# A PEER feed-forward kernel on one Trainium2 core: the gates of the last two token blocks are handed to the first expert tiles on chip, gate flushes run on across token tiles, and 40 activation tiles are spilled in place of 42

## The chip, the core and the metric

The kernel runs on one core of one Trainium2 chip. The metric is the device time of one execution in microseconds (us). The kernel before takes 3240.67 us, the median of 3 runs (3237.8 to 3242.23).

## What is computed

A trunk of two residual layers on 512 tokens of width 1024. Each layer has a token mixer (attention with pooling, then attention with a recurrence) and a PEER feed-forward: 8 heads choose 16 of 16,384 single-neuron experts for each token. Only this last part is touched:

```python
q  = (xt @ w_query).reshape(n_tok, 8, 2, 128)
s1 = einsum('thd,nd->thn', q[:, :, 0], sub_k1); s2 = einsum('thd,nd->thn', q[:, :, 1], sub_k2)
v1, i1 = top_k(s1, 16); v2, i2 = top_k(s2, 16)          # first-level choice
cand = v1[..., :, None] + v2[..., None, :]
top_s, pos = top_k(cand.reshape(n_tok, 8, 256), 16)     # second-level choice
idx  = take_along_axis(i1 * 128 + i2, pos); gate = softmax(top_s)
act  = gelu(einsum('thkd,td->thk', expert_u[idx], x))
out  = einsum('thk,thkd->td', gate * act, expert_v[idx])
```

## The kernel before

The function `peer` does this part in each layer. For 384 of the 512 tokens (three token tiles of 128) it computes all 16,384 experts densely, as 128 expert tiles of 128 experts; the last 128 tokens gather the rows of their chosen experts one by one (`g_fetch`, `g_work`, lines 1721 to 1747).

**u side.** `u_step(j)` makes the activations of expert tile j: it fetches the weights of tile j+5 (`ur`, SP's queue, line 1359), rounds those of tile j+3 (`uh`, ACT), makes the remainder of tile j+2 (`ul`, DVE, line 1374), runs 24 matmuls of 384 columns on PE (lines 182 to 184) and takes the gelu on ACT. The first 12 tiles stay on chip; the next `NB_SPILL` are written to memory (`ad`, line 1385) and read back on the v side; the rest are made there.

**Second-level choice and gates.** `level2(t)` (lines 1500 to 1567) makes the chosen pairs and gates of token tile t on DVE. It ends with three PE transposes into `pkT`, which ACT copies to `pT`. `gates(t)` (lines 1569 to 1611) spreads them over all experts in 8 blocks of 16 tokens. For each block DVE builds four one-hot tensors (`ohC`, `ohA`, `ohB` twice, line 1604); a `flush` is 8 small matmuls on PE into `gps` (line 1587) and one copy by ACT into `gs` (line 1589); four flushes fill a block, which ACT's queue then writes to memory (`gd`, line 1591). Flushes trail by up to four, and each `gates(t)` empties its list before it returns (lines 1608 and 1609).

**The order around it.** `background()` is a hand-written interleaving. Every piece of `level2` and `gates` yields a cost; after each 4.2 of cost (`G_STEP`) one `u_step` is put in, up to `NB_ACT + NB_SPILL - NB_LAST` = 49. Pieces of `level2(t+1)` are mixed into `gates(t)` (line 1619). Steps 49 to 51 follow, then the pools of this stage are closed (line 1640) and the v side takes their memory.

**v side.** `V(j)`, as the text calls `v_mm(j)`, is 18 matmuls of 512 columns on PE into six accumulators (line 1704). It needs `vh` and `vl` (`v_load`: fetched `vr`, rounded on ACT, remainder on DVE) and `Hh` and `Hl` (`h_make`: activation times gate, `Hf`, on DVE line 1685, then split). The gates come back from memory as `gt`, for 8 expert tiles at a time (`g_load`, line 1656). Ahead of the loop stand `g_load(0)` with all 24 blocks, three `vr` fetches, `v_load(0)`, step 52, `h_make(0)` and step 53. In round j below 42 of the loop only V(j) runs on PE; after that each round has a u step and a V. `units` spreads the gathered rows of the last tokens over the rounds.

Every transfer of the SP and ACT queues takes the next of eight completion counters in turn, and its issue waits until the transfer eight places before it has landed.

Of the kernel before, what the change touches and what calls it, by code (L numbers as in the profile page):

```python
# [1316 lines left out]
GJ = 8  # L1317
G_STEP = 4.2
NB_ACT = 12
NB_SPILL = 42  # L1320
ROWS = 5
ADA_M = 12
TAIL = NE - 2
NB_LAST = 5


def peer(k, layer):
    nc, tc = k.nc, k.tc
    I = k.I
    with ExitStack() as st:  # L1330
# [20 lines left out]

        up = st.enter_context(tc.tile_pool(name="pu", bufs=2, reuse_waits="tile"))
        ap = st.enter_context(tc.tile_pool(name="pact", bufs=NB_ACT, reuse_waits="tile"))
        U, ACTS = {}, {}

        def u_fetch(j):
# [128 lines left out]
        nc.vector.tensor_copy(IF, IX)  # L1485
        wk = tk.enter_context(tc.tile_pool(name="pwk", bufs=1, reuse_waits="tile"))
        psG = tk.enter_context(tc.tile_pool(name="psG", bufs=6, space=PSUM, reuse_waits="tile"))
        PK = {}

        def tree(m, out):  # L1490

# [8 lines left out]
        def level2(t):  # L1500
            v1, v2 = V[:, t, 0], V[:, t, 1]
            x1, x2 = IF[:, t, 0], IF[:, t, 1]
            cand = wk.tile([P, 8, NCAND], F32, name="cand")
            d1 = wk.tile([P, 8, 16], F16, name="d1")
            nc.vector.tensor_tensor(d1[:, :, 1:16], x1[:, :, 1:16], x1[:, :, 0:15], op=ALU.subtract)
            nc.vector.tensor_copy(d1[:, :, 0:1], x1[:, :, 0:1])
            o = 0
            for a0, na, nb in SEGS:
                dst = cand[:, :, o:o + na * nb].rearrange("p h (a b) -> p h a b", a=na)
                nc.vector.tensor_tensor(dst, bc(v1[:, :, a0:a0 + na, None], [P, 8, na, nb]),  # L1510
                                        bc(v2[:, :, None, 0:nb], [P, 8, na, nb]), op=ALU.add)
                o += na * nb
            yield 2.0
            tv = wk.tile([P, 8, 16], F32, name="tv")
            tp = wk.tile([P, 8, 16], U32, name="tp")
            cr = wk.tile([P, 8, NCAND], F32, name="cr")
            for h in (0, 4):
                top16([(tv[:, i], tp[:, i], cand[:, i, :], cr[:, i, :]) for i in range(h, h + 4)])
                yield 2.4
            d1x = wk.tile([P, 16, 8, 16], F16, name="d1x", tag="dx")  # L1520
            k.act(d1x, bc(d1.rearrange("p h a -> p a h")[:, :, :, None], [P, 16, 8, 16]), AF.Copy)
            pk = wk.tile([P, 3, P], F32, name="pk", bufs=2)
            ge = wk.tile([P, 8, 16], F32, name="ge")
            nc.vector.tensor_tensor(ge, tv, bc(tv[:, :, 0:1], [P, 8, 16]), op=ALU.subtract)
            k.act(ge, ge, AF.Exp)
            pf = wk.tile([P, P], F16, name="pf")
            nc.vector.tensor_copy(pf, tp.rearrange("p h k -> p (h k)"))

            c1 = wk.tile([P, 16, P], F16, name="c1")
            m1 = wk.tile([P, 16, P], F16, name="m1")  # L1530
            nc.vector.tensor_tensor(c1, bc(pf[:, None, :], [P, 16, P]), startx, op=ALU.is_ge)
            yield 1.6
            nc.vector.tensor_tensor(m1, c1, d1x.rearrange("p a h k -> p a (h k)"), op=ALU.mult)
            yield 1.1
            tree(m1, pk[:, 0])
            yield 1.3
            x2x = wk.tile([P, 16, 8, 16], F16, name="x2x", tag="dx")
            k.act(x2x, bc(x2.rearrange("p h a -> p a h")[:, :, :, None], [P, 16, 8, 16]), AF.Copy)
            nc.vector.tensor_tensor(m1, c1, dsx, op=ALU.mult)
            yield 1.1  # L1540
            bb = wk.tile([P, P], F16, name="bb")
            tree(m1, bb)
            nc.vector.tensor_tensor(bb, pf, bb, op=ALU.subtract)
            yield 1.5
            nc.vector.tensor_tensor(c1.rearrange("p a (c t) -> p a c t", t=2),
                                    bc(bb.rearrange("p (c t) -> p c t", t=2)[:, None], [P, 16, 64, 2]),
                                    bc(iotax[:, 0:16, None, :], [P, 16, 64, 2]), op=ALU.is_equal)
            yield 1.1
            nc.vector.tensor_tensor(m1, c1, x2x.rearrange("p a h k -> p a (h k)"), op=ALU.mult)
            yield 1.1  # L1550
            tree(m1, pk[:, 1])
            gs = wk.tile([P, 8], F32, name="gs")
            nc.vector.tensor_reduce(gs, ge, axis=AX.X, op=ALU.add)
            nc.vector.reciprocal(gs, gs)
            nc.vector.tensor_scalar(gs, gs, GSCALE, None, op0=ALU.mult)
            nc.vector.tensor_tensor(pk[:, 2].rearrange("p (h k) -> p h k", h=8), ge, bc(gs[:, :, None], [P, 8, 16]),
                                    op=ALU.mult)
            yield 2.0
            PK[t] = pk
            if t < NTD:  # L1560

                ps = psG.tile([P, 4, P], F32, name="pkT", tag="g")
                for i in range(3):
                    nc.tensor.transpose(ps[:, i, :], pk[:, i], cst(k, "ident"))
                pT = wk.tile([P, 4, P], F16, name="pT", bufs=2)
                k.act(pT[:, 0:3], ps[:, 0:3], AF.Copy)
                PK[t] = (pT, ps)

        def gates(t):
# [7 lines left out]
            pT, ps = pk  # L1577
            nc.vector.tensor_tensor(pT[:, 3], ps[:, 2], pT[:, 2], op=ALU.subtract)
            yield 0.3
            pend = []  # L1580

            def flush():
                A, B, gs, blk, q = pend.pop(0)
                ps = psG.tile([P, 4, P], F32, name="gps", tag="g")
                for i in range(4):
                    for r in range(2):
                        nc.tensor.matmul(ps[:, i, :], A[:, 2 * q + i // 2, :, i % 2], B[r][:, 2 * q + i // 2, :, i % 2],  # L1587
                                         start=r == 0, stop=r == 1, skip_group_check=True)
                k.act(gs[:, :, 4 * q:4 * q + 4].rearrange("p j t -> p t j"), ps, AF.Copy, scale=1.0 / GSCALE)
                if q == GB // 4 - 1:  # L1590
                    nc.scalar.dma_start(gd[blk], gs)


            iota = bc(iotax[:, None], [P, GB // 2, P, 2])
            for b in range(P // GB):
                gs = wk.tile([P, NE, GB], F32, name="gs_", bufs=2)
                C, A = (wk.tile([P, GB // 2, P, 2], F16, name=nm, bufs=n) for nm, n in (("ohC", 1), ("ohA", 3)))
                B = [wk.tile([P, GB // 2, P, 2], F16, name="ohB", bufs=4) for _ in range(2)]

                def pt(i):  # L1600
                    return bc(pT[:, i, b * GB:b * GB + GB].rearrange("p (q t) -> p q t", t=2)[:, :, None, :], [P, GB // 2, P, 2])

                for out, a, i, op in ((C, iota, 1, ALU.is_equal), (A, iota, 0, ALU.is_equal), (B[0], C, 2, ALU.mult), (B[1], C, 3, ALU.mult)):
                    nc.vector.tensor_tensor(out, a, pt(i), op=op)
                    if len(pend) > 3:
                        flush()
                    yield 1.2
                pend += [(A, B, gs, t * (P // GB) + b, q) for q in range(GB // 4)]
            while pend:
                flush()  # L1610
            yield 0.1

        def background():
            yield from level2(0)
            for t in range(3):
                g = level2(t + 1)
                for i, cost in enumerate(gates(t)):
                    yield cost
                    if 12 * (i + 1) // 31 > 12 * i // 31:
                        yield next(g, 0.0)  # L1620
                yield from g
            yield from gates(3)
# [8 lines left out]
        for cost in background():  # L1631
            debt += cost
            if debt >= G_STEP and ju < NB_ACT + NB_SPILL - NB_LAST:
                debt -= G_STEP
                u_step(ju)
                ju += 1
        while ju < NB_ACT + NB_SPILL - 2:
            u_step(ju)
            ju += 1
        tk.close()  # L1640


        with ExitStack() as st2:
            vp = st2.enter_context(tc.tile_pool(name="pv", bufs=2, reuse_waits="tile"))
            psO = st2.enter_context(tc.tile_pool(name="psO", bufs=1, space=PSUM, reuse_waits="tile"))
            O_ = [[psO.tile([P, 512], F32, name=f"o{t}{b}") for b in range(2)] for t in range(NTD)]
            VV, GG, HH = {}, {}, {}

            def g_load(j, parts):

# [31 lines left out]
            def h_make(j):  # L1682
                g = GG[j // GJ]
                hf = vp.tile([P, TD], F32, name="Hf", bufs=1)
                nc.vector.tensor_tensor(hf.rearrange("p (b t) -> p b t", t=GB),
                                        ACTS.pop(j).rearrange("p (b t) -> p b t", t=GB), g[:, :, j % GJ, :], op=ALU.mult)
                if j == NE - 1:

                    h, l = (up.tile([P, TD], F32R, name="acts", bufs=3) for _ in range(2))
# [14 lines left out]
                            mm(O_[t][b], w[:, ts], v[:, 512 * b:512 * b + 512], start=s, stop=e, skip_group_check=True)  # L1704


            acc = vp.tile([P, D], F32, name="gacc", bufs=1)
            nc.vector.memset(acc, 0.0)
            ops = []
            for c in range(P + 20):  # L1710
# [100 lines left out]
                nc.sync.dma_start(k.O["out_0_dram"][t * P:t * P + P, :], o)  # L1811


            g_load(0, range(6))
            for _ in range(3):
                v_fetch()
            v_load(0)
            while ju < NB_ACT + NB_SPILL:
                if ju == NB_ACT + NB_SPILL - 1:
                    h_make(0)  # L1820
                u_step(ju)
                ju += 1
# [230 lines left out]
```

## Time and profile before

| | |
|---|---|
| median of 3 runs | 3240.67 us |
| the profiled execution, its own time | 3234.92 us |
| its span, first to last instruction | 3233.2 us |
| PE busy | 3125.4 us, 97% |
| DVE busy | 2421.7 us, 75% |
| ACT busy | 1410.6 us, 44% |
[...]
| share of PE in the chain that ended last | 84% |

PE is busy almost everywhere, so a change shows where PE waits or runs at a lower clock. The views below are: busy time of each engine in a stretch, waits (who waited for whom), the timeline of one engine, the chain that ended last, and the landing times of transfers. Layer 0's stage of gates ends near 652 us and its v side begins at 686.5 us; in layer 1 the same places are near 2338 and 2373 us.

### The profile page before, as it was taken

Reading aid. Unit: us, or ns where it says so; the run is one execution under the profiler, and the core shown is the slowest. Engines: PE = TensorE matmul, PEld = TensorE weight load, DVE = VectorE, ACT = ScalarE, POOL = GpSimd, SP = SyncE. Lnnn points to the kernel's source line nnn. Section 1 sums busy time; section 2 is a strip of 40 time slices with the busy share of each in tenths; the row PEclk is TensorE's granted clock in tenths of the full one; section 3 lists DMA queues with packets and bytes.
Section 4 is the critical chain, followed back from the end, with each engine's and each line's share of the span. In section 5 each row is a group of like instructions: output and inputs, shape, how many; then the busy total and the mean of one; then the engine's idle time right before and its main releaser. Section 6 shows DMA issues by size and latency. Waiting matters only on the chain.

```text
span 3233.2 us, 55219 instructions
## 1 busy us (share of the span) xinstructions
PE 3125.4 (97%) x21696; PEld 2736.8 (85%) x21696; DVE 2421.7 (75%) x4749; ACT 1410.6 (44%) x1959; POOL 856.8 (27%) x671
## 2 busy tenths in 40 slices
PE   7999999989999999999999899999989999999998
PEld 5777899978899999997677787899978899999997
DVE  5255799957888888887565456899957888888886
ACT  3253367743333333333444533367733333333334
POOL 0002200013444444442020103100013344444442
PEclk8999999999999999999999999999999999999999
DMA  8523246789999999995521014256799999999994
GB/s 313 209 92 139 99 159 248 249 306 349 331 331 343 334 336 331 336 337 178 209 67 53 6 61 163 95 183 231 265 316 342 328 336 338 337 333 333 341 328 146
DMA packets 321830, 794.27 MB, mean 246 GB/s; under 512 B 26400, under 2 KB 162976, under 8 KB 309280
## 3 DMA queue, kind: packets, MB, share of 16 engines
q1 hardware_dynamic: 225968, 439.53, 39.5%
q0 software_dynamic: 75008, 274.78, 24.1%
q10 hardware_dynamic: 20592, 76.43, 6.3%
q8 instruction: 170, 2.79, 0.4%
q14 instruction: 92, 0.75, 0.1%
HBM read 715.36 MB, written 75.24 MB: 245 GB/s over the span
## 4 chain that ended last, share of the span: by engine, by line
PE 84%; DVE 8%; ACT 3%; DMA 3%; issue 2%; ACTq 0%; POOL 0%; DVEq 0%; SPq 0%
PE o L1704 31%; PE ups L182 9%; PE ups L184 9%; PE ups L183 9%; PE bk L182 3%; PE bk L184 3%; PE bk L183 3%; PE bk L745 2%; PE gps L1587 2%; PE qps L182 2%; PE adaps L242 1%; PE qps L183 1%; PE qps L184 1%; PE qps L429 1%; DVE ul L1374 1%
## 5 line engine op out<-in xcount | busy, mean ns | idle before, releaser
L182 PE MATMUL ups<-phh,uh 128*128 128x384 f32 x2048 | 694.6, 339 | 0.0
L184 PE MATMUL ups<-phh,ul 128*128 128x384 f32 x2048 | 689.3, 337 | 0.0
L183 PE MATMUL ups<-phl,uh 128*128 128x384 f32 x2048 | 687.9, 336 | 0.0
L1726 POOL DMA_INDIRECT row<-peer_u,xres x256 | 348.1, 1360 | 1098.1 <-PE gps L1587 552.7
L151 ACT ACTIVATE vh<-vr 128x1024 fp32r<-128x1024 f32 x254 | 269.9, 1063 | 553.7 <-issue 457.0
L1704 PE MATMUL o<-vh,Hh 128*128 128x512 f32 x1524 | 475.1, 393 | 20.7 <-ACT Hh L151 20.6
L1704 PE MATMUL o<-vl,Hh 128*128 128x512 f32 x1524 | 472.7, 391 | 0.0
L1704 PE MATMUL o<-vh,Hl 128*128 128x512 f32 x1524 | 472.4, 391 | 0.0
L1726 POOL DMA_INDIRECT row<-peer_v,xres x256 | 342.9, 1340 | 417.8 <-DVE xres L1742 330.1
L182 PEld LDWEIGHTS ups<-phh,uh 128*128 128x128 f32 x2048 | 386.5, 189 | 5.8
L176 DVE TENSOR_TENSOR vl<-vr,vh 128x1024 fp32r<-128x1024 f32 x254 | 311.1, 1225 | 107.1 <-ACT vh L151 102.6
L183 PEld LDWEIGHTS ups<-phl,uh 128*128 128x128 f32 x2048 | 386.3, 189 | 5.8
L184 PEld LDWEIGHTS ups<-phh,ul 128*128 128x128 f32 x2048 | 385.9, 188 | 0.8 <-DVE ul L1374 0.6
L1704 PEld LDWEIGHTS o<-vh,Hh 128*128 128x128 f32 x1524 | 284.0, 189 | 72.9 <-ACT Hh L151 24.0
L1704 PEld LDWEIGHTS o<-vl,Hh 128*128 128x128 f32 x1524 | 287.3, 189 | 62.6
L1704 PEld LDWEIGHTS o<-vh,Hl 128*128 128x128 f32 x1524 | 287.0, 188 | 61.7
L1374 DVE TENSOR_TENSOR ul<-ur,uh 128x1024 fp32r<-128x1024 f32 x256 | 311.7, 1217 | 30.8 <-ACT uh L151 22.1
L1745 DVE SCALAR_TENSOR_TENSOR gacc<-row,xres,gacc 128x1024 f32<-128x1024 f32 x256 | 327.5, 1279 | 0.8
L176 DVE TENSOR_TENSOR Hl<-Hf,Hh 128x384 fp32r<-128x384 f32 x254 | 141.9, 559 | 242.0 <-ACT Hh L151 242.0
L1742 DVE SCALAR_TENSOR_TENSOR xres<-row,xres 128x1024 f32<-128x1024 f32 x256 | 311.6, 1217 | 0.0
L151 ACT ACTIVATE uh<-ur 128x1024 fp32r<-128x1024 f32 x256 | 269.5, 1053 | 27.9 <-DMA ur<-peer_uT 13.6
L151 ACT ACTIVATE act<-ups 128x384 f32<-128x384 f32 x172 | 84.5, 491 | 367.5 <-PE ups L184 367.5
(475 smaller groups left out, 4500.0 us busy)
## 6 DMA issues: line engine op xcount, KB each, us to landing
ur<-peer_uT SPq DMA_DIRECT2D x256, 512.0 KB, 7.0
vr<-peer_vp SPq DMA_DIRECT2D x256, 512.0 KB, 6.6
gt<-gd SPq DMA_DIRECT2D x180, 256.0 KB, 7.7
adaw<-ada_w SPq DMA_DIRECT2D x32, 1024.0 KB, 6.7
ad<-acts ACTq DMA_DIRECT2D x84, 192.0 KB, 3.7
act<-ad SPq DMA_DIRECT2D x84, 192.0 KB, 6.8
wraw<-od_w_in SPq DMA_DIRECT2D x30, 512.0 KB, 3.6
wraw<-peer_wq SPq DMA_DIRECT2D x26, 512.0 KB, 4.1
```

Source lines behind the costliest of these rows:

```text
L151: return self.nc.scalar.activation(out, in_, func, **kw)
L176: (eng or k.nc.vector).tensor_tensor(lo, src, hi.bitcast(F32), op=ALU.subtract)
L182: mm(out, w[0], x[0], start=start, stop=False, skip_group_check=True)
L183: mm(out, w[0], x[1], start=False, stop=False, skip_group_check=True)
L184: mm(out, w[1], x[0], start=False, stop=stop, skip_group_check=True)
L745: mm(ps[h, a, :], l(h, a), r(h, a), start=start and a == 0, stop=stop, skip_group_check=True)
L1374: nc.vector.tensor_tensor(l, r, h.bitcast(F32), op=ALU.subtract)
L1587: nc.tensor.matmul(ps[:, i, :], A[:, 2 * q + i // 2, :, i % 2], B[r][:, 2 * q + i // 2, :, i % 2], start=r == 0, stop=r == 1, skip_group_c ...
L1704: mm(O_[t][b], w[:, ts], v[:, 512 * b:512 * b + 512], start=s, stop=e, skip_group_check=True)
L1726: nc.gpsimd.indirect_dma_start(out=r, out_offset=None, in_=I[f"peer_{kind}{layer}"], in_offset=bass.IndirectOffsetOnAxis(ap=eidx[:, c:c + ...
L1742: nc.vector.scalar_tensor_tensor(junk, r, 1.0, htok, op0=ALU.mult, op1=ALU.mult, accum_out=dots[:, c:c + 1])
L1745: nc.vector.scalar_tensor_tensor(acc, r, wts[:, c:c + 1], acc, op0=ALU.mult, op1=ALU.add)
```

## The change

- `NB_SPILL` 42 to 40 and `NB_LAST` 5 to 3: the bound on steps in the background stays at 49, but only steps 49, 50 and 51 follow, all behind the closing of the pools; two u steps move into the loop of the v side.
- `glate`, a small tile that outlives the stage: when the last two blocks (22 and 23) are flushed, GpSimd copies the gates of expert tiles 0 to 7 from `gs` into it. The first `gt` load covers blocks 0 to 21 alone, and `h_make` of tiles 0 to 7 multiplies in two pieces.
- The list of pending flushes lives across token tiles; it is emptied only after the last, behind one more yield of `G_STEP`.
- Pieces of `level2(t+1)` are mixed in denser (13 per 27 in place of 12 per 31), and its transposes come one piece later.
- `gacc`, the first `gt`, `vr` and `row` are placed first in the v side's memory. `gt` 0 lies, as before, over tiles of the second-level choice; the first `vr` lies over such tiles too, the second and third `vr` reach into the first `gs` buffer, `row` lies over both `gs` buffers and some one-hots (before: over one-hots alone), `vh` and `vl` over one-hots (before: over `gs`).
- `v_load(0)` and `h_make(0)` both stand before the last u step ahead of the loop.

```diff
-NB_SPILL = 42
+NB_SPILL = 40
-NB_LAST = 5
+NB_LAST = 3
+NLATE = 2
...
+        glate = ap.tile([P, NLATE, GJ, GB], F32, name="glate", bufs=1)
...
-        PK = {}
+        PK, pend = {}, []
...
             PK[t] = pk
+            yield 0.0
             if t < NTD:
...
-            pend = []
...
                 if q == GB // 4 - 1:
                     nc.scalar.dma_start(gd[blk], gs)
+                    if blk >= TD // GB - NLATE:
+                        nc.gpsimd.tensor_copy(glate[:, blk - TD // GB + NLATE], gs[:, 0:GJ, :])
...
-                pend += [(A, B, gs, t * (P // GB) + b, q) for q in range(GB // 4)]
-            while pend:
-                flush()
-            yield 0.1
+                pend.extend((A, B, gs, t * (P // GB) + b, q) for q in range(GB // 4))
+            if t == NTD - 1:
+                yield G_STEP
+                while pend:
+                    flush()
+                yield 0.1
...
-                    if 12 * (i + 1) // 31 > 12 * i // 31:
+                    if 13 * (i + 1) // 27 > 13 * i // 27:
                         yield next(g, 0.0)
...
-        while ju < NB_ACT + NB_SPILL - 2:
-            u_step(ju)
-            ju += 1
         tk.close()
...
+            acc = vp.tile([P, D], F32, name="gacc", bufs=1)
+            GG[0] = vp.tile([P, TD // GB, GJ, GB], F32, name="gt")
+            for nm, n in (("vr", 3), ("row", ROWS)):
+                vp.tile([P, D], F32, name=nm, bufs=n)
...
-                nc.vector.tensor_tensor(hf.rearrange("p (b t) -> p b t", t=GB),
-                                        ACTS.pop(j).rearrange("p (b t) -> p b t", t=GB), g[:, :, j % GJ, :], op=ALU.mult)
+                a, f = (x.rearrange("p (b t) -> p b t", t=GB) for x in (ACTS.pop(j), hf))
+                n = TD // GB - (NLATE if j < GJ else 0)
+                nc.vector.tensor_tensor(f[:, :n], a[:, :n], g[:, :n, j % GJ, :], op=ALU.mult)
+                if j < GJ:
+                    nc.vector.tensor_tensor(f[:, n:], a[:, n:], glate[:, :, j, :], op=ALU.mult)
...
-            g_load(0, range(6))
+            nc.sync.dma_start(GG[0][:, :TD // GB - NLATE], gd[:TD // GB - NLATE, :, 0:GJ, :].rearrange("b p j t -> p b j t"))
             for _ in range(3):
                 v_fetch()
-            v_load(0)
             while ju < NB_ACT + NB_SPILL:
                 if ju == NB_ACT + NB_SPILL - 1:
+                    v_load(0)
                     h_make(0)
```

How the order of instructions moves is shown at three places of layer 0. A row is a line, an operation, out<-in, the size and how many follow each other.

**ACT at the turn from token tile 0 to 1.** `gs` rows are flush copies, `uh` and `acts` belong to a u step. Before:

```order
L151 ACTIVATE pT<-pkT 128x384
L151 ACTIVATE gs__5095<-gps 128x4x128
L1591 DMA gd<-gs__5095 128x2048
L151 ACTIVATE gs__5180<-gps 128x4x128 x4
L1591 DMA gd<-gs__5180 128x2048
L151 ACTIVATE gs__5311<-gps 128x4x128 x4
L1591 DMA gd<-gs__5311 128x2048
L151 ACTIVATE uh<-ur 128x1024
```

The change:

```order
L151 ACTIVATE pT<-pkT 128x384
L151 ACTIVATE gs__5012<-gps 128x4x128
L1593 DMA gd<-gs__5012 128x2048
L151 ACTIVATE uh<-ur 128x1024
L151 ACTIVATE acts<-ups 128x384
L1387 DMA ad<-acts 128x384
L151 ACTIVATE gs__5098<-gps 128x4x128 x3
L151 ACTIVATE uh<-ur 128x1024
L151 ACTIVATE acts<-ups 128x384
L1387 DMA ad<-acts 128x384
L151 ACTIVATE gs__5098<-gps 128x4x128
L1593 DMA gd<-gs__5098 128x2048
```

The run of eight copies without a u step between them is broken into threes and ones.

**SP's queue, from the last u weights of the stage to the first rounds of the v side.** Before:

```order
L1359 DMA ur<-peer_uT 128x1024 x53
L1656 DMA gt<-gd 128x24x128
L1666 DMA vr<-peer_vp 128x1024 x3
L1656 DMA gt<-gd 128x4x128
L1666 DMA vr<-peer_vp 128x1024
L1359 DMA ur<-peer_uT 128x1024 x2
```

The change:

```order
L1361 DMA ur<-peer_uT 128x1024 x50
L1824 DMA gt<-gd 128x22x128
L1674 DMA vr<-peer_vp 128x1024 x3
L1361 DMA ur<-peer_uT 128x1024 x2
L1664 DMA gt<-gd 128x4x128
L1674 DMA vr<-peer_vp 128x1024
```

`gt` moves ahead of three fetches of u weights, two of which now stand between the third `vr` and the second `gt`.

**ACT from the last flushes to V(1).** Before, from the last u step ahead of the first `vh`; block 23's write (`gs__7245`) stands three more u steps further up:

```order
L151 ACTIVATE uh<-ur 128x1024
L151 ACTIVATE acts<-ups 128x384
L1385 DMA ad<-acts 128x384
L151 ACTIVATE vh<-vr 128x1024
L151 ACTIVATE uh<-ur 128x1024
L151 ACTIVATE acts<-ups 128x384
L1385 DMA ad<-acts 128x384
L151 ACTIVATE Hh<-Hf 128x384
L151 ACTIVATE uh<-ur 128x1024
L151 ACTIVATE acts<-ups 128x384
L1385 DMA ad<-acts 128x384
L151 ACTIVATE vh<-vr 128x1024
```

The change, from block 23 (`gs__7246`) on:

```order
L151 ACTIVATE gs__7246<-gps 128x4x128 x4
L1593 DMA gd<-gs__7246 128x2048
L151 ACTIVATE uh<-ur 128x1024
L151 ACTIVATE acts<-ups 128x384
L1387 DMA ad<-acts 128x384
L151 ACTIVATE uh<-ur 128x1024
L151 ACTIVATE acts<-ups 128x384
L1387 DMA ad<-acts 128x384
L151 ACTIVATE vh<-vr 128x1024
L151 ACTIVATE Hh<-Hf 128x384
L151 ACTIVATE uh<-ur 128x1024
L151 ACTIVATE acts<-ups 128x384
```

Four u steps lie between block 23 and the first `vh` before, two in the change, and the one between the first `vh` and the first `Hh` is gone.

## Rows read from the trace of the kernel before

**Rows 1.** Busy time by stretch, layer 0: us, then busy time and count on PE, PEld (weight loads), DVE, ACT and POOL, granted clock, DMA share, GB/s. The first stretch lies in the stage of gates, the second at the head of the v side.
```profile
560.00:620.00 60.00, 59.11 (x477) 57.33 (x476) 59.46 (x131) 46.33 (x54) 0.00 (x0) 1.00 0.73 253
700.00:740.00 40.00, 40.00 (x178) 33.05 (x177) 29.98 (x44) 15.89 (x20) 13.23 (x8) 1.00 0.87 302
```
**Rows 2.** The chain that ended last, pieces of the mixed rounds of layer 0: start, us, what. Between two V there is one u step.
```profile
864.60 4.12 PE o L1704 x18
872.91 4.12 PE o L1704 x18
```
**Rows 3.** Waits of PE over the whole span: us in total, times, longest.
```profile
PE o L1704 <- ACT Hh L151: 20.6, 6, 9.0
PE gps L1587 <- DVE ohB L1604: 8.7, 9, 2.8
...
PE gps L1587 <- DVE pT L1578: 1.5, 2, 0.8
```
**Rows 4.** The same for the stretch 660 to 700 us (layer 0), then 2340 to 2380 us (layer 1).
```profile
PE o L1704 <- ACT Hh L151: 9.0, 1, 9.0
...
PE o L1704 <- ACT Hh L151: 8.9, 1, 8.9
```
**Rows 5.** Busy time by stretches of 5 us, columns as in Rows 1: layer 0, then layer 1.
```profile
685.00:690.00 5.00, 3.50 (x8) 2.84 (x9) 3.32 (x5) 2.90 (x4) 0.00 (x0) 0.50 0.94 293
690.00:695.00 5.00, 5.00 (x21) 4.01 (x20) 2.27 (x4) 1.58 (x2) 0.00 (x0) 0.87 0.93 297
695.00:700.00 5.00, 5.00 (x24) 4.15 (x23) 2.85 (x5) 1.59 (x2) 0.00 (x0) 1.00 0.80 250
...
2370.00:2375.00 5.00, 1.73 (x4) 1.44 (x5) 4.36 (x5) 3.03 (x6) 0.00 (x0) 0.50 0.61 188
2375.00:2380.00 5.00, 5.00 (x18) 3.94 (x18) 2.25 (x3) 1.86 (x3) 0.00 (x0) 0.75 0.90 303
```
**Rows 6.** Timeline of SP's queue, layer 0: start, us, what. A row of several spans them all.
```profile
644.85 21.86 SPq L1359 DMA_DIRECT2D ur<-peer_uT  x6
667.40 0.39 SPq L1656 DMA_DIRECT2D gt<-gd  x1
670.32 7.49 SPq L1666 DMA_DIRECT2D vr<-peer_vp  x3
```
**Rows 7.** Waits of SP's queue from 600 to 700 us.
```profile
SPq L1666 <- DMA ad<-acts: 2.5, 1, 2.5
```
**Rows 8.** The chain that ended last, from 650 to 700 us: start, us, what.
```profile
670.32 11.57 DMA vr<-peer_vp
```
**Rows 9.** Transfers issued from 640 to 700 us: size, median us from issue to landing. `gs__7029`, `gs__7114` are blocks 21 and 22.
```profile
ur<-peer_uT SPq DMA_DIRECT2D x8, 512.0 KB, 6.4
vr<-peer_vp SPq DMA_DIRECT2D x7, 512.0 KB, 5.2
...
gt<-gd SPq DMA_DIRECT2D x1, 1536.0 KB, 13.2
...
gd<-gs__7029 ACTq DMA_DIRECT2D x1, 1024.0 KB, 4.7
gd<-gs__7114 ACTq DMA_DIRECT2D x1, 1024.0 KB, 9.0
...
row<-peer_u,xres POOLq DMA_INDIRECT x5, 14.5
```
**Rows 10.** Timeline of ACT, layer 0, from the last flushes to V(2): start, us, what, idle before it and its releaser.
```profile
652.71 0.33 ACTq L1591 DMA_DIRECT2D gd<-gs__7114  x1
...
656.89 0.33 ACTq L1591 DMA_DIRECT2D gd<-gs__7245  x1
...
658.28 0.47 ACT L151 ACTIVATE acts<-ups 128x384 f32<-128x384 f32 x1
...
659.21 1.06 ACT L151 ACTIVATE uh<-ur 128x1024 fp32r<-128x1024 f32 x1 [0.46 <-ACT acts L151]
...
681.97 1.06 ACT L151 ACTIVATE vh<-vr 128x1024 fp32r<-128x1024 f32 x1 [11.09 <-DMA vr<-peer_vp]
...
693.15 1.06 ACT L151 ACTIVATE vh<-vr 128x1024 fp32r<-128x1024 f32 x1 [1.64 <-PE o L1704]
695.97 0.53 ACT L151 ACTIVATE Hh<-Hf 128x384 fp32r<-128x384 f32 x1 [1.76 <-DVE Hf L1685]
```
**Rows 11.** Timeline of DVE behind the turn from token tile 0 to 1: layer 0, then layer 1.
```profile
512.37 1.23 DVE L1374 TENSOR_TENSOR ul<-ur,uh 128x1024 fp32r<-128x1024 f32 x1 [3.59 <-ACT uh L151]
...
2199.24 1.22 DVE L1374 TENSOR_TENSOR ul<-ur,uh 128x1024 fp32r<-128x1024 f32 x1 [5.35 <-ACT uh L151]
```
**Rows 12.** Timeline of PE at the same two places.
```profile
514.79 0.56 PE L1587 MATMUL gps<-ohB,ohA 128*128 128x128 f16 x7 [0.94 <-DVE ohB L1604]
...
2201.66 0.56 PE L1587 MATMUL gps<-ohB,ohA 128*128 128x128 f16 x7 [2.76 <-DVE ohB L1604]
```
**Rows 13.** Timeline of PE at the end of the last flushes of layer 0; the second row is the first matmul of the next u step.
```profile
650.55 1.94 PE L1587 MATMUL gps<-ohB,ohA 128*128 128x128 f16 x31 [0.72 <-DVE ohB L1604]
652.29 0.42 PE L182 MATMUL ups<-phh,uh 128*128 128x384 f32 x1
```
**Rows 14.** Timeline of DVE there: the last one-hot of layer 0.
```profile
649.28 1.21 DVE L1604 TENSOR_TENSOR ohB<-ohC,pT 128x2048 f16<-128x2048 f16 x1
```
**Rows 15.** Groups of instructions on POOL: the nearest to a copy of 128x128.
```profile
L1778 POOL TENSOR_TENSOR vr<-vr 128x128 f32<-128x128 f32 x6 | 2.7, 456 | 0.5
```

More of the change, by code (lines that the diff above doesn't have):

```diff
@@ L1704, in v_mm @@
                             mm(O_[t][b], w[:, ts], v[:, 512 * b:512 * b + 512], start=s, stop=e, skip_group_check=True)
-            acc = vp.tile([P, D], F32, name="gacc", bufs=1)
             nc.vector.memset(acc, 0.0)
```

## The prediction, on record before the changed kernel ran

> **What bounds the kernel now.** I read the busy time by stretch first: in the stage of gates PE is busy 59.1 of 60 us with DVE at 59.5, and on the v side PE is busy all of 40 us [rows 1]. So PE sets the time, and only its waits and its clock can be won. Of its waits [rows 3] the largest is 20.6 us, for `Hh`; two stretches hold 9.0 and 8.9 us of it [rows 4], once per layer, just ahead of V(0). Waits of the flush matmuls for one-hots and `pT` add 8.7 + 1.5 us [rows 3].
>
> The long wait also lowers the clock. Behind it the granted clock is 0.50 and then 0.87 (0.50 and 0.75 in layer 1), against 1.00 and 24 matmuls per 5 us soon after [rows 5]. At 24 per 5 us the 3.50 us busy would have held 16.8 matmuls and held 8, the next 5 us held 21: 11.8 short, 2.4 us. In layer 1 1.73 us held 4 for 8.3, then 18 for 24: 10.3 short, 2.1 us. **The turn to the v side costs 9.0 + 2.4 and 8.9 + 2.1, in all 22.4 us.**
>
> Why the wait is there: SP issued six fetches of u weights until 666.7, then `gt` at 667.40 and the first `vr` at 670.32 [rows 6]. The `vr` had to wait for an `ad` transfer [rows 7], its landing took 11.57 us [rows 8], and ACT stood still 11.09 us for it, at 681.97 [rows 10]. The last flush had left PE at 652.3 [rows 13]; the six u steps behind it lasted until about 677.4 (6 x 4.19, below).
>
> **Price of a u step.** V(j) starts 8.31 us apart in the mixed rounds and takes 4.12 [rows 2], which leaves 4.19 for a u step. All 128 u steps and 128 V per layer remain; two u steps per layer move into mixed rounds, where PE is the bound. That moves 8.4 us from one side of V(0) to the other and gains nothing. Two spilled tiles fewer save four transfers of 192 KB per layer, beside a full PE: nothing.
>
> **The turn, rebuilt.** Let E be the end of the last flush on PE. In the change three u steps follow it: PE is free for V(0) at E + 12.6.
> - U(50) ends at E + 8.4. From a gelu to ACT's next `uh` it is 0.9 us (658.28 to 659.21), from the start of `vh` to that of `Hh` 2.8 (693.15 to 695.97), then 0.53 for `Hh` [rows 10]. V(0) could start at E + 8.4 + 0.9 + 2.8 + 0.5 = E + 12.6, plus an estimated 0.2 for the second piece of `Hf`: **0.2 us late at best.** For that `vr` must have landed at E + 9.3 and `gt` at E + 11.5.
> - `gt` needs block 21. It is flushed two u steps earlier than block 22's rest, and block 21's write took 4.7 us before [rows 9]; it is down by about E - 4. In SP's queue only one u fetch stands ahead whose buffer is freed late: by the remainder behind the last one-hot. That one-hot ended at 650.5, 1.8 us ahead of E [rows 13, 14]; with one more u step on PE ahead of E it ends up to 4 us earlier against E. So `gt` is issued between E - 4 and E + 0.5. Its landing took 13.2 us with five row fetches beside it [rows 9]; they now wait for block 23. Bounds: 13.2, and the 5.2 of a `vr` of a third of its size. I take 9, between them and nearer the half-empty case, because 2.6 MB of rows are gone. It lands at E + 5 to E + 9.5, the `vr` behind it about 1.3 later (680.6 against 681.9 before). V(0) is then late by **0.2 to 1.7 us; I take 1.2**. At 13.2 it would be up to 5.7.
> - V(1) is the next to be late. On ACT its `vh` stands behind `uh` of tile 54, and that fetch stands on SP behind the second `vr`, which now waits for block 22's write. That write starts near E + 0.4, as before (652.71 against 652.3) [rows 10, 13], and took 9.0 then, block 21's 4.7 [rows 9]: I take 6.6. Two places on the queue later the u fetch goes out at E + 8 and lands 6.4 later [rows 9], at E + 14; `uh` and gelu take 1.9, `vh` to the start of V 3.4: V(1) at E + 19. V(0) ends at E + 12.6 + 1.2 + 4.1 = E + 17.9. **Late by about 1 us**; with 9.0 and 11.57 for the two landings, by up to 9.
> - The clock: the stretch of gates, with its short waits, shows 1.00 [rows 1]; I keep 0.8 per layer for the chance that waits of 1 us lower it here.
>
> So the turn costs 2 x (1.2 + 1.0 + 0.8) = 6 us in place of 22.4: **16.4 us won.**
>
> [...]
>
> **The gates.** At the turn from token tile 0 to 1 ACT copies eight flushes in a row; the next `uh` is late and DVE waits 3.59 and 5.35 us for it [rows 11]. PE then waits 0.94 and 2.76 for a one-hot [rows 12] and twice 0.8 for `pT` [rows 3]. The copies are now spread among u steps and `pT` comes earlier, so I count these 5.3 us as won. The bounds are nothing won (new waits elsewhere in the interleaving) and all 10.2 of the two rows; DVE, nearly as full as PE, is late next.
>
> **Small additions.** 16 more DVE pieces of 128x32 lie beside a full PE, but for the 0.2 above. Two copies on POOL per layer, some 0.46 us each by the nearest row [rows 15], have 8 us until `h_make(0)` reads them. Behind them on POOL stand the row fetches, first needed four rounds into the v side.
>
> **Sum.** 16.4 + 5.3 = 21.7 us. The profiled execution, 3234.9, would become 3213; the median stands 5.8 above it, so the forecast is 3240.7 - 21.7 = **3219 us**.
>
> **Rivals.** A measurement of this kernel tells about 0.2% from no change, 6.5 us.
> 1. **A second wait takes the first one's place** at V(1): block 22's write and the u fetch land as slowly as the worst rows, and V(1) is late by 9 us with 2.3 us of low clock. For it: the DMA engines are busy 0.94 of the time at the turn [rows 5]. Against it: the rows are out of the way. It costs 2 x (9 + 2.3 - 1.8) = 19 more: 3238.
> 2. **Slower: the row fetches collide with the head of the v side.** They wait for block 23's write and go out near E + 12, when `vr`, `gt` parts and spilled tiles must stream. That stretch has 302 GB/s at 0.87 of the engines [rows 1]; 2.6 MB more (five row fetches of 512 KB) over 18 us is 145, in all 447, some 100 over what 0.87 allows for (302/0.87 = 347): 1.8 MB behind, 5.2 us. If that falls on rival 1's late start, PE loses 9 + 5.2 and twice a low clock of 2.3, with 1.2 at V(0): 20 us per layer against 11.2 + 2.7 won. 2 x 6.1 = 12 us slower: 3253. It decides from 13.9 us lost per layer. [...]
> 3. **The change does not free SP's queue**: the u fetch ahead of `gt` is held and `gt` goes out no earlier against V(0) than now. The turn stays as it is and only gates gain: 3235.
>
> **Chances.** Forecast (3210 to 3228) 0.68; rival 1, with all between it and the forecast, 0.16; rival 3 0.06; rival 2 0.10. The best case is 0.5 us per turn and all 10.2 of gates, 3240.7 - 31.6 = 3209. The upper end reaches past rivals 3 to most of rival 1, 3237; rival 2 and the worst of rival 1 stay out. Faster takes the forecast and half of rival 1 (those under 3234): 0.76. Same: the rest of rival 1 and rival 3, 0.14. Slower: 0.10.
>
> **What would show it.** In the profile after: PE's wait for `Hh` under 5 us in total; no stretch at the turn with a clock of 0.5; `gt` issued within 2 us of the last flush, ahead of the last u fetch; ACT's 11.09 us wait gone; DVE's 3.59 and 5.35 us gone. It is wrong if a wait of over 5 us stands before V(1) or V(2), or if PE's waits for one-hots grow over 10 us.

## The result and the profile after

The changed kernel takes **3220.38 us** (median of 6 runs, 3217.72 to 3226.1) against 3240.63 for the kernel before (6 runs on the same chip): ratio 0.9944, 95% interval 0.9934 to 0.9954, 20.3 us less by the medians. The forecast was 3219 with a range of 3209 to 3237. The total came out as forecast; its two terms did not. The turn won less than half of what was forecast and the gates twice as much.

The profiled execution took 3222.18 us, with a span of 3220.4, 12.8 less than the span before. The difference is smaller than that of the medians because the profiled execution of before was 5.7 us faster than its median and this one is 1.8 slower. Part of it lies where the change touches nothing: from the last expert tile of layer 0 to the first transposes of layer 1 this trace has 596.0 us (1511.7 to 2107.7), the one before 590.9 (1520.4 to 2111.3). Of these 5.1 us, 3.3 are PE's wait for `ada_w`, 3.8 here and 0.5 before.

Waits of PE over the whole span, as in [rows 3] (us in total, times, longest):

```profile
PE o L1715 <- ACT Hh L151: 14.2, 7, 5.2
...
PE pkT L1567 <- DVE pk L1500: 6.5, 3, 2.9
...
PE adaps L242 <- DMA Nr<-ada_w: 3.8, 1, 3.8
...
PE pkT L1567 <- DVE pk L1558: 2.4, 4, 0.6
...
PE gps L1589 <- DVE ohB L1608: 1.6, 2, 0.8
```

The wait for `Hh` fell from 20.6 to 14.2, not to under 5. Waits for one-hots fell from 8.7 to 1.6 and those for `pT` are gone; those of the transposes for `pk` grew from 6.8 (two groups, 5.7 and 1.1) to 8.9. The same waits by place, as in [rows 4], in 640 to 690 us and 2330 to 2380 us:

```profile
PE o L1715 <- ACT Hh L151: 5.2, 1, 5.2
...
PE o L1715 <- ACT Hh L151: 6.2, 2, 4.5
```

In layer 0 it is V(0) that waits. In layer 1 V(0) waits 1.7 (6.2 - 4.5) and V(1) 4.5. The stretches of 5 us there, columns as in [rows 5], layer 0 and then layer 1:

```profile
660.00:665.00 5.00, 4.21 (x25) 3.89 (x23) 0.00 (x0) 0.49 (x1) 0.00 (x0) 1.00 0.97 389
665.00:670.00 5.00, 0.64 (x2) 0.55 (x3) 2.48 (x5) 1.58 (x2) 3.73 (x4) 0.71 1.03 398
670.00:675.00 5.00, 5.00 (x15) 3.96 (x14) 2.82 (x4) 2.70 (x4) 1.56 (x2) 0.60 1.03 409
675.00:680.00 5.00, 5.00 (x23) 4.13 (x22) 2.88 (x5) 1.90 (x3) 0.00 (x0) 1.00 1.04 397
...
2355.00:2360.00 5.00, 3.63 (x9) 2.90 (x10) 3.43 (x8) 2.00 (x3) 0.00 (x0) 0.67 1.04 406
```

The clock is low again behind the wait (0.60 in layer 0, 0.67 in layer 1): 15 matmuls where 24 fit in 5 us, and 9 where 17.4 fit in 3.63 (with 23 of 24 in the next 5 us). Counted as in the prediction this is 2.1 and some 2.0 us. The DMA engines are full (0.97 to 1.04, near 400 GB/s) in all these stretches.

SP's queue and the `vr` that was late, as in [rows 6] (timeline) and then [rows 8] (chain of waits):

```profile
649.22 0.39 SPq L1824 DMA_DIRECT2D gt<-gd  x1
649.67 12.37 SPq L1674 DMA_DIRECT2D vr<-peer_vp  x3
662.13 2.43 SPq L1361 DMA_DIRECT2D ur<-peer_uT  x2
```
```profile
649.67 16.15 DMA vr<-peer_vp
```

`gt` goes out at 649.22, 2.3 us ahead of the end of the last flush (651.5), as forecast. The first `vr`, issued 0.45 later, needed 16.15 us. ACT and its queue from there, as in [rows 10], layer 0 and then layer 1:

```profile
652.22 0.33 ACTq L1593 DMA_DIRECT2D gd<-gs__7162  x1
...
656.40 0.33 ACTq L1593 DMA_DIRECT2D gd<-gs__7246  x1
...
665.84 1.06 ACT L151 ACTIVATE vh<-vr 128x1024 fp32r<-128x1024 f32 x1 [5.27 <-DMA vr<-peer_vp]
...
670.02 1.06 ACT L151 ACTIVATE uh<-ur 128x1024 fp32r<-128x1024 f32 x1 [0.72 <-DMA ur<-peer_uT]
...
2344.02 1.06 ACT L151 ACTIVATE vh<-vr 128x1024 fp32r<-128x1024 f32 x1 [1.85 <-DMA vr<-peer_vp]
...
2351.07 1.06 ACT L151 ACTIVATE uh<-ur 128x1024 fp32r<-128x1024 f32 x1 [3.63 <-DMA ur<-peer_uT]
```

The first two rows are the writes of blocks 22 and 23, of 1 MB each: they go out behind `gt` and ahead of the landing of that `vr`. In the kernel before block 23's write went out at 656.89 [rows 10] and took 10.4 us, so both had landed when `gt` was issued at 667.40. ACT's 11.09 us became 5.27 and 1.85. In layer 1 the u weights of tile 54 are late as well, and V(1)'s `vh` stands behind them on ACT: the place of rival 1, at some half of its price.

The first u step behind the flushes, by its first matmul, and V(0) (timeline of PE, layer 0), as in [rows 13]:

```profile
651.48 0.42 PE L182 MATMUL ups<-phh,uh 128*128 128x384 f32 x1
...
669.36 1.22 PE L1715 MATMUL o<-vh,Hh 128*128 128x512 f32 x2 [5.15 <-ACT Hh L151]
```

The flushes end 0.8 us earlier than before (652.29 in [rows 13]) although one more u step of 4.19 us stands ahead of them: some 5 us won in the gates of layer 0.

### The profile page after: what moved, and what is told of

It is laid out like the page before. It is cut to its first block, busy times and chain, and to the rows that moved or that the text cites. A ratio compares the mean times of both kernels' runs of the same rounds, so it can differ in the third digit from the quotient of the medians.

```text
span 3220.4 us, 55222 instructions
## 1 busy us (share of the span) xinstructions
PE 3123.0 (97%) x21696; PEld 2733.1 (85%) x21696; DVE 2417.3 (75%) x4765; ACT 1411.7 (44%) x1959; POOL 873.7 (27%) x675
## 4 chain that ended last, share of the span: by engine, by line
PE 77%; DVE 14%; issue 3%; ACT 3%; DMA 3%; ACTq 0%; POOL 0%; DVEq 0%; SPq 0%
PE o L1715 31%; PE ups L182 7%; PE ups L184 7%; PE ups L183 7%; PE bk L182 3%; PE bk L184 3%; PE bk L183 3%; DVE ohB L1608 2%; PE bk L745 2%; DVE ul L1376 2%; PE qps L182 2%; PE adaps L242 2%; PE qps L184 1%; PE qps L183 1%; PE qps L429 1%
## 5 line engine op out<-in xcount | busy, mean ns | idle before, releaser
L1715 PE MATMUL o<-vh,Hh 128*128 128x512 f32 x1524 | 475.3, 393 | 14.2 <-ACT Hh L151 14.2
L1715 PEld LDWEIGHTS o<-vh,Hh 128*128 128x128 f32 x1524 | 283.5, 188 | 66.7 <-ACT Hh L151 18.4
```

## The experiments

Each kernel was timed in five rounds against the kernel before, the change in the runs above. Ratios are to that kernel, with 95% intervals; 0.001 is 3.2 us.

| kernel | median, us | ratio | PE's waits for `Hh` in its trace |
|---|---|---|---|
| the change | 3220.4 | 0.9944 (0.9934 to 0.9954) | 14.2 |
| e1 gates only | 3233.1 | 0.9970 (0.9958 to 0.9982) | 24.3 |
| e2 head only | 3237.4 | 0.9993 (0.9984 to 1.0002) | 18.4 |
| e7 e2 and the yield | 3233.6 | 0.9978 (0.9969 to 0.9987) | 16.5 |
| e12 e7 and dense mixing | 3230.9 | 0.9974 (0.9964 to 0.9985) | 17.4 |
| e11 e7 and carried flushes | 3225.4 | 0.9957 (0.9943 to 0.9972) | 17.6 |
| e8 no handing over | 3240.7 | 1.0000 (0.9991 to 1.0009) | 34.0 |
| e3 `vr` first | 3223.0 | 0.9942 (0.9928 to 0.9955) | 14.7 |
| e6 rows later | 3219.7 | 0.9932 (0.9919 to 0.9946) | 12.7 |
| e9 free queue | 3221.0 | 0.9941 (0.9927 to 0.9954) | 10.5, and 4.6 at V(1) without a releaser |
| e4 42 and 5 | 3217.9 | 0.9924 (0.9911 to 0.9938) | 4.3 |
| e5 u ahead of `vr` | 3220.5 | 0.9936 (0.9922 to 0.9950) | 10.8 |
| e10 free queue, 42 and 5 | 3213.9 | 0.9916 (0.9903 to 0.9930) | 6.8 |

### The two halves: e1 and e2

e1 is the kernel before with these lines of the change alone:

```diff
-        PK = {}
+        PK, pend = {}, []
...
+            yield 0.0
...
-            while pend:
-                flush()
-            yield 0.1
+            if t == NTD - 1:
+                yield G_STEP
+                while pend:
+                    flush()
+                yield 0.1
...
-                    if 12 * (i + 1) // 31 > 12 * i // 31:
+                    if 13 * (i + 1) // 27 > 13 * i // 27:
```

> The kernel before with the scheduling of the gates alone: pending flushes live across token tiles, one more yield behind the last one-hot, transposes one piece later, 13 pieces per 27. Memory, spilled tiles and the head of the v side stay as before. Theory A (from the trace of the change: the last flush came 4.9 and 6.6 us earlier against the same number of u steps): 11 us of the 20 are won here, 3229 to 3231 us. Rival B (the prediction's terms): 5.3 us, 3235. Rival C: nothing is kept, because the head of the v side waits for vr at a fixed time after the last flush's step count, 3240.

e2 is the change with those lines as before.

> The change without the scheduling of the gates: pending flushes are emptied in each token tile, 12 pieces per 31, transposes as before; the two late blocks handed over on chip, the memory order, 40 spilled tiles and the order at the head stay. Theory A: the turn alone wins 6 to 9 us, 3232 to 3235. Rival B (the prediction's term): 16.4 us, 3224. In the trace: with one u step fewer ahead of the last flush, gt goes out no earlier than in the change, and PE waits for Hh 9 us or more over both layers.

Measured: 0.9970 and 0.9993. The halves win 9.7 and 2.3 us, 12 together, where both win 18 (by the ratios); e2's interval holds 1. By its median (3233.1) e1 lies between its theories A and B, by its ratio (3230.9 us) in the range of A; e2 wins less than either of its theories. What each lacks is in ACT's row at the turn of layer 0, in e1 and then in e2:

```profile
678.99 1.06 ACT L151 ACTIVATE vh<-vr 128x1024 fp32r<-128x1024 f32 x1 [13.71 <-DMA vr<-peer_vp]
```
```profile
673.60 1.06 ACT L151 ACTIVATE uh<-ur 128x1024 fp32r<-128x1024 f32 x1 [10.48 <-DMA ur<-peer_uT]
```

In e1 the flushes end earlier, but `gt` goes out at 667.33 (667.40 before): ACT waits 13.71 us in place of 11.09, and PE's waits for `Hh` rise to 24.3. So the turn takes back a part of what the gates win. In e2 only 48 u steps stand ahead of the last flush, as before; the u weights of tile 53 then stand behind three `vr` fetches on SP, the last two of which wait until block 22 is written, `vh` stands behind their `uh` on ACT, and V(0) waits 8.0 us. The new order of the memory and the place of `v_load(0)` were not tried by themselves.

### What couples them: e7, e11, e12

e7 is e2 and one line of the change:

```diff
+            if t == NTD - 1:
+                yield G_STEP
             while pend:
                 flush()
```

> The kernel e2_head_only (flushes emptied in each token tile) with one thing back: the yield of one u step behind the last one-hot of the last token tile. In e2 the u weights of tile 52 stand on SP behind vr fetches that wait for block 22's write, and ACT waited 10.48 us for them; with one more u step ahead of the last flush that fetch stands ahead of gt. Theory A (this one yield is what couples the two parts): the turn wins 5 to 7 us over e2, 3230 to 3232. Rival B (the coupling comes from the carried flushes): as e2, 3236 to 3238.

(The tile is 53, not 52.) Measured 0.9978, 4.9 us better than e2 by the ratios and 3.9 by the medians, with intervals that overlap a little: nearer to theory A, with a little less won than it says. ACT's wait of 10.48 us for the u weights became 0.57. The other lines of the gates were then tried apart on e7: e11 has the carried flushes (`pend` across token tiles), e12 the mixing of 13 per 27 with the later transposes.

> The change with the old mixing of the second-level choice (12 pieces per 31, transposes at the old place); flushes still live across token tiles. With e7_head_yield (neither, 3233.6) and the change (both, 3220) it splits the gates' part. Theory A (the eight copies in a row on ACT behind each token tile are what made one-hots late): most of the 13 us is won here, 3222 to 3225. Rival B (the denser mixing and the later transposes do it): 3230 to 3233.

> The other half: the denser mixing (13 pieces per 27) and the later transposes, with the flushes emptied in each token tile and the one yield behind the last one-hot. Theory A: little is won, 3230 to 3234, and PE's waits for one-hots behind the token tiles stay near 7 us. Rival B: most of it, 3222 to 3226.

Measured 0.9957 and 0.9974. Carrying the flushes wins 6.8 us over e7; mixing denser 1.3, which can't be told from nothing: theory A in both, with 3225.4 for e11 just above its range. Both together, the change, win 11. The traces give the same order: from the first transposes to the first matmul behind the last flush, layer 0 takes 229.4 us in e7, 228.7 in e12, 226.2 in e11 and 225.4 in the change. Waits of PE for one-hots in e7, e11 and e12, then waits of DVE for `uh` in the stage of gates of layer 0 (426 to 652 us), in e7 and e12; e11 and the change have none:

```profile
PE gps L1590 <- DVE ohB L1609: 7.7, 6, 2.7
```
```profile
PE gps L1588 <- DVE ohB L1607: 1.8, 2, 0.9
```
```profile
PE gps L1591 <- DVE ohB L1610: 5.1, 5, 1.8
```
```profile
DVE ul L1376 <- ACT uh L151: 3.5, 1, 3.5
```
```profile
DVE ul L1376 <- ACT uh L151: 4.0, 1, 4.0
```

### The handing over: e8

```diff
-                    if blk >= TD // GB - NLATE:
-                        nc.gpsimd.tensor_copy(glate[:, blk - TD // GB + NLATE], gs[:, 0:GJ, :])
...
-            nc.sync.dma_start(GG[0][:, :TD // GB - NLATE], gd[:TD // GB - NLATE, :, 0:GJ, :].rearrange("b p j t -> p b j t"))
+            nc.sync.dma_start(GG[0], gd[:, :, 0:GJ, :].rearrange("b p j t -> p b j t"))
```

and one multiplication in `h_make`.

> The change without the handing over: gt covers all 24 blocks, h_make multiplies in one piece, no copies on GpSimd; everything else stays. gt must then wait until block 23 is written, which was issued at 656.40 in the change, 7 us later than gt's issue there, and took 4.7 to 9.0 us before. Theory A: gt lands 12 to 16 us later and V(0) with it, the low clock comes back: 2 x 13, 3244 to 3250. Rival B (V(0) waits for vr and u weights anyway, whose places on the queue do not change): 5 us or less, 3221 to 3226.

Measured 1.0000: the whole gain is gone. The mechanism is that of theory A; the time, some 20 us above the change, is just below its range. SP's and PE's waits in it, the first from 640 to 700 us:

```profile
SPq L1819 <- DMA gd<-gs__7246: 13.0, 1, 13.0
```
```profile
PE o L1710 <- ACT Hh L151: 34.0, 6, 15.7
```

`gt` goes out at 660.25, 11 us later than in the change; V(0) is 15.7 and 15.6 us late. All that the gates win is lost again there. It is the handing over together with the cover that counts: e1 has no handing over either, but keeps the five u steps behind the last flush, and wins 9.7 us.

### What is left at the turn: e3, e6, e9

e3 changes the order on SP:

```diff
+            v_fetch()
             nc.sync.dma_start(GG[0][:, :TD // GB - NLATE], ...)
-            for _ in range(3):
+            for _ in range(2):
                 v_fetch()
```

> The change with the first vr fetch put ahead of gt on SP's queue. In the change the first vr needed 16.15 us from issue to landing behind gt, and V(0) of layer 0 waited 5.2 us for it; gt was needed only one step later. Theory A (order on a full set of DMA engines decides): vr lands some 8 us earlier, gt at most 1.5 us later, V(0) waits 2 us less or more per layer, 3213 to 3217. Rival B (bytes decide: gt, two block writes and u weights fill the engines until about 664 whatever the order, and gt then ends last): no change, 3219 to 3222.

e6 takes the rows out of the turn:

```diff
-            g_fetch(3)
+            dly = vp.tile([P, 1], F32, name="dly", bufs=1)
...
                 h_make(j + 1)
+                if j == 1:
+                    nc.gpsimd.tensor_copy(dly, HH[j][0][:, 0:1].bitcast(F32))
+                    g_fetch(3)
...
-            units = [0 if j < 4 else ...
+            units = [0 if j < 6 else ...
```

> The change with the five row fetches held back until the second Hh of the v side is made (some 10 us later than in the change), and their work two rounds later. Theory A (the head waits for transfers queued on SP behind other waits, and the rows go out after the first vr has landed): no change, 3218 to 3222. Rival B (bytes: 2.6 MB less beside the u weights and the vr of V(1)): V(1)'s wait of 4.5 us in layer 1 and the low clock go, 3212 to 3216.

e9 frees SP's queue of its waits:

```diff
-                    nc.scalar.dma_start(gd[blk], gs)
+                    (nc.gpsimd if blk >= TD // GB - NLATE else nc.scalar).dma_start(gd[blk], gs)
...
+            vp.tile([P, D], F32, name="vr", bufs=3)
             GG[0] = vp.tile([P, TD // GB, GJ, GB], F32, name="gt")
-            for nm, n in (("vr", 3), ("row", ROWS)):
-                vp.tile([P, D], F32, name=nm, bufs=n)
+            vp.tile([P, D], F32, name="row", bufs=ROWS)
```

> The change with every wait of SP's queue at the turn taken away: the vr buffers lie ahead of gt in memory (no longer over a gs_ buffer), and the last two blocks are written by GpSimd's queue, so that no vr or u fetch stands behind a block's write or its completion counter. gt, three vr and the u weights of tiles 53 and 54 can then go out between 649 and 653. Theory A (the waits left at the turn are waits in SP's queue): V(1)'s wait goes, V(0) waits 2 us or less per layer, 3211 to 3215. Rival B (bytes: 6 MB must pass between 649 and 665 in either case): the u weights and vr land about as late as in the change, V(0) as late as before (5 us) or later since three vr now stand beside gt, 3218 to 3224.

None of the three differs from the change (0.9942, 0.9932, 0.9941). e6: V(0) still waits 4.6 and 5.3 us, so the rows were not what held it; in the change the first of them goes out at 665.36, when the first `vr` has all but landed. In layer 1 of e6 V(1)'s wait is gone, but V(0)'s is 5.3 in place of 1.7. Rival 2's collision doesn't show in the time. e3 and e9 did what they were to do and it didn't help. SP's fetches of u weights and ACT's `uh` of tile 54 in e3, then in e9:

```profile
662.05 2.37 SPq L1361 DMA_DIRECT2D ur<-peer_uT  x2
...
669.39 1.06 ACT L151 ACTIVATE uh<-ur 128x1024 fp32r<-128x1024 f32 x1 [3.50 <-DMA ur<-peer_uT]
```
```profile
653.98 4.49 SPq L1361 DMA_DIRECT2D ur<-peer_uT  x2
...
669.12 1.06 ACT L151 ACTIVATE uh<-ur 128x1024 fp32r<-128x1024 f32 x1 [3.67 <-DMA ur<-peer_uT]
```

In e9 these weights go out 8.1 us earlier than in the change (653.98 against 662.13) and are there 0.9 us earlier (669.12 against 670.02; the last flush of e9 ends 0.4 us earlier too). V(0) starts 3.4 us earlier in e3 (665.9) and 3.9 in e9 (665.5), and V(1) then waits for tile 54's `uh` ahead of it on ACT: 4.4 us in e3 and 4.6 in e9. The latter has no releaser in the profile and so does not stand among the waits for `Hh`:

```profile
PE o L1715 <- issue: 4.6, 1, 4.6
```

This is what rival B says: with the DMA engines full (e9: busy 0.95 to 1.02, 376, 421 and 390 GB/s from 655 to 670), the weights that went out 8.1 us earlier were there 0.9 us earlier, as if they had to let the bytes ahead of them pass. That it is the volume on which the head hangs is a reading and not shown: no run takes the block writes or `gt` away.

### More cover: e4, e5, e10

e4 is the change with `NB_SPILL = 42` and `NB_LAST = 5`: the two u steps of 4.19 us that the change moved behind V(0) stand ahead of it again.

> The change with 42 spilled tiles and a bound five short of the end, as before: five u steps in place of three lie between the last flush and V(0), everything else of the change stays. Theory A (the waits of 5.2, 1.7 and 4.5 us ahead of V(0) and V(1), and the low clock behind them, are only missing cover): two steps of 4.19 us cover them, 10 to 15 us less than the change, 3206 to 3211. Rival B (landings move along with the u fetches on the same queue, or four more transfers of 192 KB cost what the cover wins): within 3 us of the change, 3217 to 3223.

Measured 0.9924: 2.5 us better than the change by the medians, 6.5 by the ratios, with intervals that overlap a little. By time that is rival B. In the trace it is half of A: the wait for `Hh` falls to 4.3, but a u step now waits, since the u weights of tile 54 (not 52) are as late as ever. e4 differs from e1 by the new head and memory order alone, and wins 15 us over it: with the cover kept, the head is worth most of the 16.4 that the prediction gave the turn. ACT's timeline, then PE's waits over the span:

```profile
671.95 1.06 ACT L151 ACTIVATE uh<-ur 128x1024 fp32r<-128x1024 f32 x1 [9.26 <-DMA ur<-peer_uT]
```
```profile
PE ups L182 <- ACT acts L151: 5.3, 2, 3.0
```

e5 puts the second and third `vr` of e4 behind the u weights:

```diff
-            for _ in range(3):
-                v_fetch()
+            v_fetch()
...
+                    v_fetch()
+                    v_fetch()
                     v_load(0)
                     h_make(0)
```

> The kernel with 42 spilled tiles and five u steps behind the last flush (e4_42_5), with the second and third vr fetch put behind the last four fetches of u weights on SP's queue. In e4 ACT waited 9.26 us for the u weights of tile 52, because the vr fetches ahead of them on the queue wait until block 22 is written, and PE waited 3.0 us for acts with the clock low behind it. Theory A (the wait that is left is a place in SP's queue): that wait goes and 2 x 4 us are won, 3208 to 3212. Rival B (the DMA engines are full at the turn, so some other transfer is as late: V(1) then waits for the second vr): within 3 us of e4, 3215 to 3221.

Measured 0.9936, no better than e4: V(1) waits 4.3 us in layer 0 and 3.4 in layer 1, now for the later `vr`. Rival B.

e10 is e9 with 42 and 5.

> The same with 42 spilled tiles and five u steps behind the last flush (the best of the runs so far was that without the free queue, 3217.9). Theory A: its waits of 9.26 us on ACT and 3.0 on PE go, with the low clock behind them, 3209 to 3213. Rival B (bytes): u weights land late beside three vr, PE waits for a u step in place of V(0), 3216 to 3222.

Measured **0.9916 (0.9903 to 0.9930), 3213.87 us, the best of all**; its interval lies just below that of the change. Against e9, on the same chip, the two more steps of cover are worth 7.1 us: its runs lie between 3207.6 and 3215.0, those of e9 between 3217.3 and 3222.9. PE over the span, and the three stretches around its V(0):

```profile
PE o L1715 <- ACT Hh L151: 6.8, 8, 1.3
...
PE ups L182 <- ACT acts L151: 3.0, 2, 1.6
```
```profile
670.00:675.00 5.00, 3.44 (x20) 3.15 (x19) 1.22 (x1) 3.77 (x5) 3.82 (x4) 1.00 0.89 303
675.00:680.00 5.00, 3.75 (x19) 3.03 (x18) 3.46 (x5) 2.77 (x5) 0.94 (x1) 1.00 1.00 350
680.00:685.00 5.00, 4.22 (x19) 3.18 (x18) 3.68 (x6) 1.77 (x3) 0.00 (x0) 1.00 1.04 409
```

No single wait at the turn is over 1.6 us and the clock stays at 1.00 through the turn: cover and early issue together do more than early issue alone (e9). Against cover alone (e4) the intervals overlap. Theory A's range (3209 to 3213) is just missed.

## Why the prediction was right, and where it was not

- **What bounds the kernel: right.** PE's waits and clock were all there was to win (PE is busy 3125.4 us before and 3123.0 in the change); the gains of the change show as fewer waits at the turn and in the gates.
- **Turn: 16.4 forecast, 7 in the trace.** Before, 22.4. After, V(0) and V(1) wait 5.2 and 1.7 + 4.5, and the clock costs 2.1 + 2.0: 15.5. The step that failed is the landing of `gt` and `vr` ("I take 9, ... because 2.6 MB of rows are gone", `vr` "about 1.3 later"). The first `vr` took 16.15 us, beyond the upper bound of 13.2 + 1.3. `gt` itself, where its landing can be read, took 14.1 to 16.0 us (e2, e4, e3, e11, e12), in place of 9. The rows had nothing to do with it (e6), and the DMA engines were as full without them (0.95 to 1.06 from 650 to 665 us in the change, where the first row goes out at 665.36). The step took the rows out from beside `gt` and did not put in the two block writes, 2 MB, that now go out behind it. Where `gt` goes out only after they have landed it took 13.2 (before) and 10.3 us (e1), though it is larger there; that the writes are the whole cause was not tried. `gt`'s issue, the other half of the step, was right.
- **V(1), 1 us: no wait in layer 0, where a late V(0) gave it time; 4.5 in layer 1**, by the mechanism that the prediction named.
- **Clock, 0.8 per layer: 2.1 and 2.0.** It followed the waits of 5.2 and 4.5 us; in e10, where no wait at the turn is over 1.6, the clock stays at 1.00.
- **u steps moved, "gains nothing": it took away cover.** True of PE's work, but a transfer was still late behind these steps: putting them back won 2.5 us (e4, not beyond its interval) or, with the queue free, 7.1 (e10 against e9).
- **Gates: 5.3 forecast, 11.5 in the trace.** From the first transposes to the last flush, 226.1 us became 225.4 in layer 0 with one more u step of 4.19, and 227.8 became 225.4 in layer 1: 4.9 + 6.6. The term took the two largest of nine waits for one-hots and counted the rest as staying, with all 10.2 of [rows 3] as its bound. The bound was the truth: in e1, where nothing else is changed, this stretch wins 4.8 + 6.3 and 0.9 us of waits for one-hots and `pT` are left. Carrying the flushes does most of it (e11): with it the waits for one-hots are gone at both turns between token tiles, not only at the first, and so is DVE's wait for `uh` behind ACT's copies, which the denser mixing leaves (e12).
- **The sum: right by luck, by two errors of opposite sign,** -9.4 and +6.2. Nor are the terms additive: with two u steps of cover gone, the gates' gain is worth nothing without the handing over (e8); without the yield the head's gain, 2 us, can't be told from nothing (e2).
- **Rivals.** 1 is real in layer 1, at some half of its price. 2 doesn't show (e6). 3 did not come; e8 shows a turn of that kind.

## What to carry to other kernels

Where the DMA engines are full, as at this turn (0.97 to 1.04), count the bytes that will be on the way beside a transfer at its new place, and not only those that it leaves behind. Issuing it earlier or in another order moved the wait to the next consumer here (e3, e9, e5); work kept ahead of the consumer (cover) removed most of it once the queue was free as well (e10: no wait over 1.6 us at the turn). Price a group of waits from its total, and ask what remains, before pricing it from its two largest rows. When two parts of a change end at the same consumer, price them together: the gain of the one is worth only what the other lets through.

## What the runs showed that was not expected

- The same stretch can have either clock, and here it made no difference. Behind the first transposes of layer 0 PE waits 2.9 us in every kernel; then the kernel before ran at 0.50, the change at 1.00 and e3, whose gates are those of the change and start at the same 426.10, at 0.66:

```profile
430.00:435.00 5.00, 4.70 (x15) 4.70 (x16) 5.00 (x15) 1.43 (x2) 0.00 (x0) 0.50 0.31 105
```
```profile
430.00:435.00 5.00, 4.81 (x28) 4.81 (x29) 5.00 (x15) 1.71 (x3) 0.00 (x0) 1.00 0.32 105
```
```profile
430.00:435.00 5.00, 4.79 (x19) 4.79 (x20) 5.00 (x15) 1.44 (x2) 0.00 (x0) 0.66 0.31 105
```

  What decides is open. 28 matmuls against 19 look like a gain, but from the first transposes to the last flush the change and e3 take the same 225.4 us, and e1, at 0.50, 225.5: DVE is busy all of the 5 us, and PE gives the time back in waits for `pk` (8.9 us over both layers in the change, 7.1 in e3).
- PE's wait for `ada_w` between the layers, which no kernel here touches, was 0.5 us in the profile of before, 1.0 in e10 and between 3.3 and 5.3 in the twelve others. With one profile of the kernel before it is open whether this is chance or something that the changed kernels bring about.
